# Two more weight blocks by seven products for their first K tile pair, and W1 over four PSUM banks

## The chip, the cores and the metric

The kernel runs on one core of one Trainium2 chip. The metric is the device time of one execution in microseconds, as the median over runs. One profiled execution is read beside it.

## What is computed

The reference is a decoder trunk of two layers over 256 tokens of width 2048, in float32. The first layer mixes by a gated short convolution, the second by latent attention; after each mixer and after each MLP stands a layer norm of `alpha * x + f(x)`. The change lies in the MLP alone, which both layers have:

```python
def sq_relu_mlp(x, w1, w2):
    return jnp.square(jax.nn.relu(x @ w1)) @ w2
```

x is 256 x 2048, W1 is 2048 x 8192, W2 is 8192 x 2048.

## The kernel before

**Products of float32.** TensorE multiplies a rounded format, so every operand is held as a high part (a cast on ScalarE, `split`, L122) and a low part (the rest, by a subtraction on VectorE, L123), and a product is three matmuls: high by high, high by low, low by high (`dot`, L284 to L286). In the W1 part the tokens' high and low parts stand side by side, so there a weight tile takes one matmul of 512 columns (`high`, L200) and one of 256 (`low`, L204).

**The weight stream.** All weights are a list of units in the order in which they are used (`stream`, `mlp_stream`). `take` hands out the next unit and prepares units ahead of it: a load on SP's queue (`load_raw`, L133) into one of 5 raw tiles, then the split into one of 8 pairs of high and low tiles. It looks ahead while the sizes of the units sum to at most `LOOK` = 5; a plain unit (128 x 1024) has size 1, a seven-product unit 3. A scheduler then decides the order of the instructions on each engine, each of which runs its queue in order.

**The MLP.** The 8192 hidden features are worked in 8 steps of 1024 features each (`for q in range(NQ)`): 8 chunks of W1, each 16 K tiles long (`products`), then W2 for these 8 K tiles. The sums of the W1 chunks take turns in PSUM banks 0 and 1. Each chunk is read out by `hidden`: a copy on ScalarE (L340), an add on VectorE (L341), relu and square on ScalarE (L654, L655), and for every second chunk the split of two K tiles and, in `form`, four sums of 128 x 128 blocks (L643 to L646) with their split. W2's output is two token tiles (t) by four blocks of 512 columns (n), kept in SBUF as `acc`.

**Seven products.** In the steps 1 to 6 (`FAST`) blocks 0 and 1 are computed by a scheme of Strassen's kind over 2 token tiles x 2 K tiles x 2 blocks: seven products of block sums in place of eight (`FACTORS`, `fast_products`). For each K tile pair, `prepare` forms the sums of W2's blocks on VectorE (L155, L158, L161) and splits them; such a unit has three pairs of high and low tiles and one of half the size (`t4`). `first_pair` runs the four K tile pairs into seven banks, which `keep` (L601) then adds into SBUF: three sums into `acc`, four ("1", "5", "7", "6", named `OWN`) into `sums`. After the last fast step, during step 7, `fold` (L620) adds `sums` into `acc`. Blocks 2 and 3 follow as plain products (`down`), one block after the other, four units each, evicted by `put` (L591). In the second MLP, `extra` adds the turned residual (L958) in steps 1 to 4.

So a fast step has these units in order: 16 plain units of W1, four seven-product units, eight plain units of W2.

Of the kernel before, what the change touches and what calls it, by code (L numbers as in the profile page):

```python
# [10 lines left out]
F32 = mybir.dt.float32  # L11
# [5 lines left out]
P = 128  # L17
W = 256 + 2
T = 256
# [15 lines left out]
NB = 4  # L35
BW = D // NB
FAST = range(1, NQ - 1)
FIRST = (0, 1, 2, 3, 4, 6, 8, 12, 16)
LEAD = 4
HEAD = 4  # L40
# [11 lines left out]
def trunk(ctx: ExitStack, tc: tile.TileContext, xT, vecs, lead, w_first, w_in, w_out, w_kv, w_q, w_uk, w_uv,  # L52
# [28 lines left out]
    def mlp_stream(l):  # L81
        out = []
        for q in range(NQ):
            out += halves(w1[l, q * QC:(q + 1) * QC])
            plain = halves(w2[l, q, 2:] if q in FAST else w2[l, q])
            fast = [(w2f[l, q, j, 0], w2f[l, q, j, 1]) for j in range(QC // 2)] if q in FAST else []
            at = 0 if q or q not in FAST else len(plain) // 2
            out += plain[:at] + fast + plain[at:]
        return out

    stream += mlp_stream(0) + halves(w_kv) + halves(w_q)
# [77 lines left out]

        return 1 if len(stream[i]) == 1 else 3  # L170

    def take(halves=2):

        i = state["next"]
        state["next"] += halves
        ahead = -sum(size(j) for j in range(i, i + halves))
        for j in range(i, len(stream)):
            ahead += size(j)
            if ahead > LOOK:
                break  # L180
# [92 lines left out]
    def products(n, x, turned=None, banks=(None,)):  # L273

        for i in range(n):
            w = take()
            ps = psum("ps_u", banks[i % len(banks)])
            mm_run([(w, ps)], x, 0, NC, NC, turned=None if i else turned)
            yield ps


    def dot(ps, w, x, first, last):

        nc.tensor.matmul(ps, x[0], w[0], start=first, stop=False)  # L284
        nc.tensor.matmul(ps, x[0], w[1], start=False, stop=False)  # L285
        nc.tensor.matmul(ps, x[1], w[0], start=False, stop=last)  # L286

    def held(x, t):
# [33 lines left out]
    OWN, KEPT = ("1", "5", "7", "6"), (2, 3, 4, 5, 6, 7, 0)  # L322
# [5 lines left out]
    def fast_products(ps, x, forms, j, n):  # L328

        b, = take(1)  # L330
        a = {"11": held(x[2 * j], 0), "12": held(x[2 * j + 1], 0), "22": held(x[2 * j + 1], 1)}
        for i in range(4):
            a[f"S{i + 1}"] = [forms[:, j, o, i * P:(i + 1) * P] for o in range(2)]
        for p, l, r in FACTORS:
            dot(ps[p], b[r], a[l], j == 0, j == n - 1)

    def whole(ps, out):

# [228 lines left out]
    def mlp(idx, ln, blocks, fast, begin=None, extra=None):  # L567
# [14 lines left out]
        def block(n, t):  # L582
            return acc[:, t, n * BW:(n + 1) * BW]
# [6 lines left out]
            else:  # L590
                nc.vector.tensor_tensor(block(n, t), block(n, t), ps, ALU.add)  # L591

        sums = fast.tile([P, 4, BW], F32, name=f"sums{idx}")

        def keep(p, ps):

            at = sums[:, OWN.index(p)] if p in OWN else block(*{"2": (0, 0), "3": (1, 0), "4": (0, 1)}[p])
            if q == 0 or q == FAST[0] and p in OWN:
                nc.scalar.copy(at, ps)
            else:  # L600
                nc.vector.tensor_tensor(at, at, ps, ALU.add)  # L601

        def first_pair(h, forms, banks):

            n = QC // 2
            ps = {p: psum(f"ps_f{p}", bank) for (p, _, _), bank in zip(FACTORS, banks)}
            for j in range(n):
                fast_products(ps, h, forms, j, n)
            for p in ps:
                keep(p, ps[p])  # L610

        def fold():

            s1, s5, s7, s6 = (sums[:, i] for i in range(4))
            both = acc[:, 1, :2 * BW].rearrange("p (b c) -> p b c", b=2)
            right = acc[:, :, BW:2 * BW]
            two = lambda v: v.unsqueeze(1).to_broadcast([P, 2, BW])
            for d, a, b in ((block(0, 0), block(0, 0), s1), (s6, s6, s1), (block(1, 0), block(1, 0), s6),
                            (s7, s7, s6), (both, both, two(s7)), (right, right, two(s5))):
                nc.vector.tensor_tensor(d, a, b, ALU.add)  # L620
                yield

        for q in range(NQ):
            ht = act.tile([P, QC, 2 * T], F32R, tag="c", name=f"h{idx}_{q}")
            h = [ht[:, k, :] for k in range(QC)]
            forms = None
            if q in FAST:
                forms = act.tile([P, QC // 2, 2, 4 * P], F32R, tag="a2", name=f"forms{idx}_{q}")
            pair = []

            def pair_tile(m):

                if m % 2 == 0:
                    pool = (act, "ab") if m % 4 else (fast, "fp")
                    t = pool[0].tile([P, 2 * T], F32, tag=pool[1], name="fp")
                    pair.append(t.rearrange("p (i t) -> p i t", i=2))
                return pair[-1]

            def form(j):
                (a11, a21), (a12, a22) = ((pair[j][:, i, :P], pair[j][:, i, P:]) for i in range(2))  # L640
                sf = fast.tile([P, 4, P], F32, tag="sf", name="sf")
                s1, s2, s3, s4 = (sf[:, i, :] for i in range(4))
                nc.vector.tensor_tensor(s1, a21, a22, ALU.add)  # L643
                nc.vector.tensor_tensor(s3, a21, a11, ALU.subtract)
                nc.vector.tensor_tensor(s2, s1, a11, ALU.subtract)
                nc.vector.tensor_tensor(s4, a12, s2, ALU.subtract)  # L646
                split(forms[:, j, 0, :], forms[:, j, 1, :], sf.rearrange("p i c -> p (i c)"))

            def hidden(m, ps, evac, *func):
                both = pair_tile(m) if q in FAST else None  # L650
                f = both[:, m % 2, :] if both is not None else tmp.tile([P, T], F32, tag="fh", name="fh", bufs=3)
                evac(ps, f, *func)
                if not func:
                    nc.scalar.activation(f, f, AF.Relu)  # L654
                nc.scalar.activation(f, f, AF.Square)  # L655
                if both is None:
                    put_split(h[m], f)
                elif m % 2:
                    at = ht[:, m - 1:m + 1, :]
                    split(at[:, :, :T], at[:, :, T:], both)  # L660
                    form(m // 2)

            if q == 0:
                for m in range(QC):
                    if m < GROUP:
                        if m == 0:
                            ws = ln.ws if ln.ws else group_of(GROUP)
                            if not ln.ws:
                                mm_wide(ws, ln.xd)
                            ln.finish()  # L670
                        ps = ws[m][1]
                    else:
                        ws = [(take(), psum("ps_w"))]
                        mm_wide(ws, ln.xd)
                        ps = ws[0][1]
                    hidden(m, ps, ln.weighted, AF.Relu)
                    if m > 0:
                        normal()
                if begin:
                    begin(range(1))  # L680
                acc = act.tile([P, 2, D], F32, tag="a1", name=f"acc{idx}")
            else:
                folds = fold()
                for m, ps in enumerate(products(QC, xhl, TURNED, (0, 1))):
                    hidden(m, ps, whole)
                    if q == NQ - 1:
                        next(folds, None)
                        if begin:
                            begin(range(max(2 * m, 1), 2 * m + 2))

            if q == NQ - 1:
                blocks(block, put, h)
                return
            if q == 0:
                for n in range(NB):
                    down(h, put, n)
            else:
                first_pair(h, forms, KEPT)
                for n, banks in ((2, (1, 2)), (3, (3, 4))):
                    down(h, put, n, banks)  # L700
                    if extra and n == 2 and q <= NB:
                        for t in range(2):
                            extra(block, q - 1, t, 5 + t)

    def to_wide(block, put, h):

# [409 lines left out]
```

## Time and profile before

| what | value |
|---|---|
| runs | median 2024.65 us (2024.43, 2024.65, 2025.12) |
| the profiled execution's own time | 2024.51 us |
| its span, first to last instruction | 2022.5 us |
| granted TensorE clock | 1.00 |
| HBM read | 381.78 MB |

In the rows of the profile, PE is TensorE's matmul, PEld its weight load, DVE VectorE, ACT ScalarE, SP the queue that issues the loads. A row of a group gives line, engine, operation, output<-inputs, shapes, count, busy us, mean ns of one, and the idle time just before with what ended it. A row of the timeline gives start and length in us. A row of the stretches gives its window, its length, and then for PE, PEld, DVE, ACT and POOL the busy time and the number of instructions, the clock, the DMA share and GB/s. Lines are those of the kernel before.

### The profile page before, as it was taken

The numbers are of one execution on the slowest core, as the hardware profiler recorded it, in microseconds if no ns is written. First come the engines' busy times: TensorE is split into PE (matmuls) and PEld (weight loads), VectorE is DVE, ScalarE is ACT, GpSimd is POOL, SyncE is SP. The second block draws the span as 40 slices with busy tenths as digits, with TensorE's granted clock in tenths as the row PEclk, the third lists the DMA queues.
The fourth block names the chain that finished last, engine by engine and source line by source line (L and its number), as shares of the span: only waits on it lengthen the run. The fifth ranks groups of instructions, "written<-read, shape, count | busy, mean of one in ns | idle before, by whom it ended". The sixth has DMA issues, their size and how long they took to land.

```text
span 2022.5 us, 30067 instructions
## 1 busy us (share of the span) xinstructions
PE 2015.9 (100%) x11240; PEld 1761.4 (87%) x11240; DVE 1605.8 (79%) x2472; ACT 1176.4 (58%) x1802; POOL 2.3 (0%) x21
## 2 busy tenths in 40 slices
PE   9999999999999999999999999999999999999998
PEld 8888888988888888888889998898888888888886
DVE  8667677788797987979688978776879798797966
ACT  6444445676565665656556655567656556565651
POOL 0000000000000000000000000000000000000000
PEclk9999999999999999999999999999999999999999
DMA  9666666564756647466654544656475664746663
GB/s 322 201 189 188 189 189 192 174 196 144 250 164 202 221 153 249 151 224 209 210 173 152 182 126 137 193 178 194 135 247 176 198 224 140 252 160 205 220 202 119
DMA packets 106849, 385.83 MB, mean 191 GB/s; under 512 B 11856, under 2 KB 12624, under 8 KB 106448
## 3 DMA queue, kind: packets, MB, share of 16 engines
q1 hardware_dynamic: 106560, 383.79, 59.5%
q8 instruction: 88, 1.44, 0.3%
q14 instruction: 57, 0.47, 0.1%
q10 hardware_dynamic: 144, 0.13, 0.0%
HBM read 381.78 MB, written 2.10 MB: 190 GB/s over the span
## 4 chain that ended last, share of the span: by engine, by line
PE 99%; DVE 0%; issue 0%; ACT 0%; DVEq 0%
PE ps_u L200 20%; PE ps_l L200 13%; PE ps_u L204 11%; PE ps_d L284 7%; PE ps_d L286 7%; PE ps_d L285 7%; PE ps_l L204 7%; PE ps_f L285 4%; PE ps_f L286 4%; PE ps_f L284 4%; PE ps_w L234 1%; PE ps_w L232 1%; PE ps_w L233 1%; PE ps_g L234 1%; PE ps_g L232 1%; PE ps_g L233 1%
## 5 line engine op out<-in xcount | busy, mean ns | idle before, releaser
L123 DVE TENSOR_TENSOR lo<-raw,hi 128x1024 fp32r<-128x1024 f32 x710 | 860.0, 1222 | 314.9 <-ACT hi L122 243.2
L122 ACT CAST hi<-raw 128x1024 fp32r<-128x1024 f32 x710 | 742.4, 1050 | 460.5 <-PE ps_u L200 107.9
L200 PE MATMUL ps_u<-xhl,hi 128*128 128x512 f32 x1792 | 621.0, 391 | 0.0
L204 PE MATMUL ps_u<-xhl,lo 128*128 128x256 f32 x1792 | 499.5, 280 | 0.0
L200 PEld LDWEIGHTS ps_u<-xhl,hi 128*128 128x128 f32 x1792 | 334.2, 187 | 72.4
L204 PEld LDWEIGHTS ps_u<-xhl,lo 128*128 128x128 f32 x1792 | 338.6, 189 | 1.8
L284 PE MATMUL ps_d<-hi,h 128*128 128x512 f32 x640 | 249.8, 390 | 0.0
L286 PE MATMUL ps_d<-hi,h 128*128 128x512 f32 x640 | 249.1, 389 | 0.0
L285 PE MATMUL ps_d<-lo,h 128*128 128x512 f32 x640 | 249.0, 389 | 0.0
L200 PE MATMUL ps_l<-xhl_a,hi 128*128 128x512 f32 x704 | 244.1, 393 | 0.0
L204 PE MATMUL ps_l<-xhl_a,lo 128*128 128x256 f32 x704 | 195.4, 279 | 0.0
L200 PEld LDWEIGHTS ps_l<-xhl_a,hi 128*128 128x128 f32 x704 | 132.1, 188 | 29.9
L286 PEld LDWEIGHTS ps_d<-hi,h 128*128 128x128 f32 x640 | 120.1, 188 | 25.0
L284 PEld LDWEIGHTS ps_d<-hi,h 128*128 128x128 f32 x640 | 120.1, 188 | 25.0 <-DVE fh L341 0.3
L285 PEld LDWEIGHTS ps_d<-lo,h 128*128 128x128 f32 x640 | 120.2, 188 | 24.7
L204 PEld LDWEIGHTS ps_l<-xhl_a,lo 128*128 128x128 f32 x704 | 131.9, 188 | 0.2
L654 ACT ACTIVATE fp<-fp 128x256 f32<-128x256 f32 x96 | 40.0, 416 | 73.7 <-DVE fp L341 72.9
L200 PE MATMUL ps_l<-z,hi 128*128 128x512 f32 x240 | 82.4, 391 | 0.0
L122 ACT CAST hi_t<-raw_t 128x1024 fp32r<-128x1024 f32 x48 | 50.4, 1050 | 42.2 <-DVE raw_t L155 33.4
L234 PE MATMUL ps_w<-xd,hi 128*128 128x258 f32 x256 | 72.8, 284 | 0.0
L232 PE MATMUL ps_w<-xd,hi 128*128 128x258 f32 x256 | 72.6, 284 | 0.0
L233 PE MATMUL ps_w<-xd,lo 128*128 128x258 f32 x256 | 72.4, 283 | 0.0
(261 smaller groups left out, 3132.3 us busy)
## 6 DMA issues: line engine op xcount, KB each, us to landing
raw<-in_w_dram SPq DMA_DIRECT2D x416, 512.0 KB, 4.4
raw<-in_w2f_dram SPq DMA_DIRECT2D x96, 512.0 KB, 3.6
raw<-in_w_in_dram SPq DMA_DIRECT2D x88, 512.0 KB, 4.3
raw<-in_w_out_dram SPq DMA_DIRECT2D x32, 512.0 KB, 3.7
raw<-in_w_o_dram SPq DMA_DIRECT2D x32, 512.0 KB, 4.2
raw<-in_w_kv_dram SPq DMA_DIRECT2D x10, 512.0 KB, 3.5
raw<-in_w_q_dram SPq DMA_DIRECT2D x8, 512.0 KB, 4.6
raw<-in_w_uk_dram SPq DMA_DIRECT2D x8, 512.0 KB, 4.6
```

Source lines behind the costliest of these rows:

```text
L122: nc.scalar.copy(hi, src)
L123: nc.vector.tensor_tensor(lo, src, hi.bitcast(F32), ALU.subtract)
L200: nc.tensor.matmul(ps, w[blk // 8][0][:, blk % 8, :], x, start=first, stop=False)
L204: nc.tensor.matmul(ps[:, :T], w[blk // 8][1][:, blk % 8, :], x[:, :T], start=False, stop=last)
L232: nc.tensor.matmul(ps[:, :W], hi, x[k][:, :W], start=k == 0, stop=False)
L233: nc.tensor.matmul(ps[:, :W], lo, x[k][:, :W], start=False, stop=False)
L234: nc.tensor.matmul(ps[:, :W], hi, x[k][:, W:], start=False, stop=k == NC - 1)
L284: nc.tensor.matmul(ps, x[0], w[0], start=first, stop=False)
L285: nc.tensor.matmul(ps, x[0], w[1], start=False, stop=False)
L286: nc.tensor.matmul(ps, x[1], w[0], start=False, stop=last)
L654: nc.scalar.activation(f, f, AF.Relu)
```

## The change

In the fast steps, blocks 2 and 3 take their first K tile pair by the seven products too (`MIXED = "sppp"`: s for seven, p for plain), and their other three pairs by plain products into the same sums where a sum is an output block ("2", "3", "4"; the fourth block, "22", begins with the plain pairs). W2's units of a step now come in the order: one seven-product unit of blocks 2 and 3, six plain units, four seven-product units of blocks 0 and 1. `sums` holds two sets of four. The W1 chunks take turns in four banks, and the banks of a step are handed on to the next in a rotation; the bank of the last chunk goes to "22". One middle matmul of a fast step (`EVEN`) is made in two halves of 256 columns. The plain W2 units are taken with a look-ahead of 6. `fold` has eight adds on 1024 columns in place of six. The host lays W2 out in pairs for all four blocks.

```diff
+MIXED = "sppp"
+EVEN = (QC - 1, "22")
...
-            plain = halves(w2[l, q, 2:] if q in FAST else w2[l, q])
-            fast = [(w2f[l, q, j, 0], w2f[l, q, j, 1]) for j in range(QC // 2)] if q in FAST else []
-            at = 0 if q or q not in FAST else len(plain) // 2
-            out += plain[:at] + fast + plain[at:]
+            if q not in FAST:
+                out += halves(w2[l, q])
+                continue
+            for j, kind in enumerate(MIXED):
+                out += [(w2f[l, q, 1, j, 0], w2f[l, q, 1, j, 1])] if kind == "s" else \
+                    halves(w2[l, q, 2, j]) + halves(w2[l, q, 3, j])
+            out += [(w2f[l, q, 0, j, 0], w2f[l, q, 0, j, 1]) for j in range(QC // 2)]
...
-    def take(halves=2):
+    def take(halves=2, look=LOOK):
...
-            if ahead > LOOK:
+            if ahead > look:
...
-    def dot(ps, w, x, first, last):
+    def dot(ps, w, x, first, last, two=False):
         nc.tensor.matmul(ps, x[0], w[0], start=first, stop=False)
-        nc.tensor.matmul(ps, x[0], w[1], start=False, stop=False)
+        for at in (slice(0, T), slice(T, 2 * T)) if two else (slice(None),):
+            nc.tensor.matmul(ps[:, at], x[0], w[1][:, at], start=False, stop=False)
         nc.tensor.matmul(ps, x[1], w[0], start=False, stop=last)
...
-        sums = fast.tile([P, 4, BW], F32, name=f"sums{idx}")
+        sums = fast.tile([P, 4, 2, BW], F32, name=f"sums{idx}")
-        def keep(p, ps):
+        def keep(p, g, ps):
-            at = sums[:, OWN.index(p)] if p in OWN else block(*{"2": (0, 0), "3": (1, 0), "4": (0, 1)}[p])
-            if q == 0 or q == FAST[0] and p in OWN:
+            at = sums[:, OWN.index(p), g, :] if p in OWN else \
+                block(*{"2": (2 * g, 0), "3": (2 * g + 1, 0), "4": (2 * g, 1), "22": (2 * g + 1, 1)}[p])
+            if q == FAST[0] and p in OWN:
...
-        def first_pair(h, forms, banks):
+        def down_pairs(h, forms, busy, free):
+            b2, b3, b4, b6 = free
+            b1, b5, b7, b22 = busy
+            ps = {p: psum("ps_d", bank) for p, bank in (("22", b22), ("3", b3), ("2", b2), ("4", b4))}
+            fresh = {"22", "3", "2", "4"}
+            for j, kind in enumerate(MIXED):
+                if kind == "s":
+                    first, last = j == MIXED.index("s"), j == MIXED.rindex("s")
+                    if first:
+                        ps.update({p: psum(f"ps_f{p}", bank) for p, bank in zip(OWN, (b1, b5, b7, b6))})
+                        fresh.update(OWN)
+                    fast_products(ps, h, forms, j, fresh, OWN if last else ())
+                    fresh &= {"22"}
+                    if last:
+                        for p in OWN:
+                            keep(p, 1, ps[p])
+                    continue
+                if extra and q <= NB and j == len(MIXED) - 1:
+                    for t in range(2):
+                        extra(block, q - 1, t, (b7, b6)[t])
+                for two in (((0, "2"), (1, "4")), ((1, "22"), (0, "3"))):
+                    w, = take(1, LOOK + 1)
+                    for t, p in two:
+                        for kk in range(2):
+                            k = 2 * j + kk
+                            dot(ps[p], wide_rows(w, kk), held(h[k], t), p in fresh, k == QC - 1, (k, p) == EVEN)
+                            fresh.discard(p)
+                    if j == len(MIXED) - 1:
+                        for _, p in two:
+                            keep(p, 1, ps[p])
             n = QC // 2
+            banks = b1, b5, b7, b6, b2, b4, b22
             ps = {p: psum(f"ps_f{p}", bank) for (p, _, _), bank in zip(FACTORS, banks)}
             for j in range(n):
-                fast_products(ps, h, forms, j, n)
+                fast_products(ps, h, forms, j, ps if j == 0 else (), ps if j == n - 1 else ())
             for p in ps:
-                keep(p, ps[p])
+                keep(p, 0, ps[p])
+            return (b3, b1, b5, b7), (b6, b2, b4, b22)
...
+        busy, free = (0, 1, 2, 3), (4, 5, 6, 7)
...
-                for m, ps in enumerate(products(QC, xhl, TURNED, (0, 1))):
+                for m, ps in enumerate(products(QC, xhl, TURNED, busy)):
...
-                first_pair(h, forms, KEPT)
-                for n, banks in ((2, (1, 2)), (3, (3, 4))):
-                    down(h, put, n, banks)
-                    if extra and n == 2 and q <= NB:
-                        for t in range(2):
-                            extra(block, q - 1, t, 5 + t)
+                busy, free = down_pairs(h, forms, busy, free)
```

More of the change, by code (lines that the diff above doesn't have):

```diff
@@ L320, in down_late, with fast_products @@
                 put(n, t, ps)
-    OWN, KEPT = ("1", "5", "7", "6"), (2, 3, 4, 5, 6, 7, 0)
+    OWN = ("1", "5", "7", "6")
     FACTORS = (("3", "S4", "22"), ("1", "11", "11"), ("5", "S1", "T1"), ("7", "S3", "T3"),
                ("2", "12", "21"), ("6", "S2", "T2"), ("4", "22", "T4"))
-    def fast_products(ps, x, forms, j, n):
+    def fast_products(ps, x, forms, j, fresh, ready):
         b, = take(1)
@@ L334, in fast_products @@
         for p, l, r in FACTORS:
-            dot(ps[p], b[r], a[l], j == 0, j == n - 1)
+            dot(ps[p], b[r], a[l], p in fresh, p in ready)
     def whole(ps, out):
@@ L614, in fold @@
             s1, s5, s7, s6 = (sums[:, i] for i in range(4))
[L615 to L619, printed above, removed]
+            c = acc.rearrange("p t (g b c) -> p t b g c", g=2, b=2)
@@ L620, in fold @@
+            for d, a, b in ((c[:, 0, 0], c[:, 0, 0], s1), (s6, s6, s1), (c[:, 0, 1], c[:, 0, 1], s6), (s7, s7, s6),
+                            (c[:, 1, 0], c[:, 1, 0], s7), (c[:, 1, 1], c[:, 1, 1], s7),
+                            (c[:, 0, 1], c[:, 0, 1], s5), (c[:, 1, 1], c[:, 1, 1], s5)):
                 nc.vector.tensor_tensor(d, a, b, ALU.add)
                 yield
+        busy, free = (0, 1, 2, 3), (4, 5, 6, 7)
         for q in range(NQ):
@@ L1095 @@
         "w2": np.stack([np.stack([_rows(q) for q in w.reshape(NQ, QC * P, D)]) for w in a["mlp_w2"]]),
-        "w2f": np.stack([np.stack([_pairs(q[:, :2 * BW]) for q in w.reshape(NQ, QC * P, D)]) for w in a["mlp_w2"]]),
+        "w2f": np.stack([np.stack([np.stack([_pairs(q[:, 2 * g * BW:2 * (g + 1) * BW]) for g in range(2)])
+                                   for q in w.reshape(NQ, QC * P, D)]) for w in a["mlp_w2"]]),
         "cosT": np.tile(cos, (4, 1)),
```

## The prediction

> **What bounds the kernel now.** I read the page first: its table of engines, the strip of slices and the chain that ended last.
>
> ```profile
> PE 2015.9 (100%) x11240; PEld 1761.4 (87%) x11240; DVE 1605.8 (79%) x2472; ACT 1176.4 (58%) x1802; POOL 2.3 (0%) x21
> PEclk9999999999999999999999999999999999999999
> PE 99%; DVE 0%; issue 0%; ACT 0%; DVEq 0%
> ```
>
> TensorE is never idle, at full clock, and the chain of work runs along it for 99% of the span. Busy time alone could hide waits inside pipelined matmuls, so I next read the table by stretches over one whole middle step of the first MLP (its W1 part, then its W2 part), a middle step of the second MLP, and the W1 part of the last step of the second MLP.
>
> ```profile
> 624.10:709.30 85.20, 85.20 (x437) 72.91 (x436) 71.70 (x96) 51.29 (x72) 0.00 (x0) 1.00 0.61 197
> 624.10:668.50 44.40, 44.40 (x258) 39.13 (x257) 34.58 (x52) 27.36 (x45) 0.00 (x0) 1.00 0.53 155
> 668.50:709.30 40.80, 40.80 (x182) 33.78 (x181) 37.12 (x45) 23.93 (x28) 0.00 (x0) 1.00 0.70 243
> 1580.90:1667.00 86.10, 86.10 (x446) 73.70 (x445) 72.86 (x98) 51.42 (x72) 0.00 (x0) 1.00 0.61 196
> 1923.60:1968.00 44.40, 44.40 (x258) 39.13 (x257) 26.85 (x34) 25.91 (x44) 0.00 (x0) 1.00 0.67 202
> ```
>
> The columns are TensorE, weight loads, VectorE and ScalarE. The W2 part holds 180 matmuls (182 with the two that straddle its borders) in 40.8 us: 0.227 us each. The timeline of TensorE gives the same from start to start; the 0.39 in each row is a latency that overlaps the next.
>
> ```profile
> 620.48 0.39 PE L286 MATMUL ps_d<-hi,h 128*128 128x512 f32 x1
> 620.70 0.39 PE L284 MATMUL ps_d<-hi,h 128*128 128x512 f32 x1
> 620.93 0.39 PE L285 MATMUL ps_d<-lo,h 128*128 128x512 f32 x1
> ```
>
> So the price of a matmul of 512 columns is 0.227 us (0.45 us over two starts), not 0.39, and a step is the bare sum of its matmuls. VectorE comes second: 71.70 of 85.20 us. It is the engine to watch.
>
> **What the change removes from TensorE.** Blocks 2 and 3 of a fast step took 8 K tiles x 2 blocks x 2 token tiles x 3 = 96 matmuls of 512 columns. With seven products for the first pair, that pair needs 7 x 3 = 21 in place of 24. There are 6 fast steps in each of 2 MLPs: 12 x 3 = 36 matmuls fewer, 36 x 0.227 = **8.17 us**.
>
> The Trainium skill ("TensorE: Matmul & The Clock Gate", section "Back-to-back issue gap") states a sustained 131 ns per matmul with N = 512; by that figure, as an estimate, the sum would be 4.7 us and the time 2020. The rows say 227 ns, and the measurement decides: no chance goes to it below.
>
> **What it adds there.** One middle matmul per fast step is split in two of 256 columns, so 12 instructions more. The nearest rows are runs of 258 columns, and one of 256 between two of 512:
>
> ```profile
> 361.99 0.28 PE L232 MATMUL ps_g<-xd,hi 128*128 128x258 f32 x1
> 362.11 0.28 PE L233 MATMUL ps_g<-xd,lo 128*128 128x258 f32 x1
> 362.23 0.28 PE L234 MATMUL ps_g<-xd,hi 128*128 128x258 f32 x1
> ...
> 624.33 0.28 PE L204 MATMUL ps_u<-xhl,lo 128*128 128x256 f32 x1
> 624.44 0.40 PE L200 MATMUL ps_u<-xhl,hi 128*128 128x512 f32 x1
> ```
>
> Start to start 0.12 and 0.11 us: two halves 0.24 against 0.227, so +0.01 each, 0.15 us in all with rounding up. Bounds: 0 (the halves stream the same columns) to a whole further slot, 12 x 0.227 = 2.7 us. I take 0.15, which the rows give nearly directly. The trace has no odd run of matmuls to tell what the split is for. The order of the rest (mixed pair, six plain units, four seven-product units) moves no matmul between stages: each step still changes from W1 to W2 work once and back once.
>
> The sum on TensorE: -8.17 + 0.15 = **-8.0 us**, if it stays fed.
>
> **What feeds it: VectorE.** Its queue is in order; each weight tile is cast high on ScalarE, then subtracted on VectorE. The rows of one seven-product unit in the step above (its first tile was subtracted before them):
>
> ```profile
> 676.22 1.22 DVE L155 TENSOR_TENSOR raw_t<-raw,raw 128x1024 f32<-128x1024 f32 x1
> 677.35 0.29 DVE L646 TENSOR_TENSOR sf<-fp,sf 128x128 f32<-128x128 f32 x1
> 677.55 0.69 DVE L158 TENSOR_TENSOR raw<-raw,raw_t 128x512 f32<-128x512 f32 x1
> 678.28 0.69 DVE L161 TENSOR_TENSOR raw<-raw 128x512 f32<-128x512 f32 x1
> 678.88 1.22 DVE L123 TENSOR_TENSOR lo_t<-raw_t,hi_t 128x1024 fp32r<-128x1024 f32 x1
> 680.02 0.69 DVE L123 TENSOR_TENSOR forms<-sf,forms 128x512 fp32r<-128x512 f32 x1
> 680.62 1.22 DVE L123 TENSOR_TENSOR lo<-raw,hi 128x1024 fp32r<-128x1024 f32 x1
> 681.76 0.68 DVE L123 TENSOR_TENSOR t<-raw,t 128x512 fp32r<-128x512 f32 x1
> 682.36 3.68 DVE L123 TENSOR_TENSOR lo<-raw,hi 128x1024 fp32r<-128x1024 f32 x3
> ...
> 690.79 1.28 DVE L601 TENSOR_TENSOR sums<-sums,ps_f 128x512 f32<-128x512 f32 x2
> ```
>
> Start to start, 1024 columns take 1.14, 512 take 0.60, 128 take 0.20 us (an eviction of 512 too: two of 0.68 in 1.28). A unit of seven products has four of 1024 (its third high-low tile among them) and three of 512: 4 x 1.14 + 3 x 0.60 = 6.36 us. It stands for two plain units of 1.14, so +4.1. The evictions rise from 11 to 15 a step: +2.4. Together +6.5 us: 71.7 becomes 78.2 of 84.5 us, 93%. That is still below TensorE, so VectorE takes no more than its idle 13.5 us; what counts is the place. ScalarE gains one cast of 1024 (1.05 us below) and one of 512, under 2 us on 51.3: covered by some 30 us of idle time. Loads stay 32 a step and only change their order in SP's queue; the look-ahead of 6 moves plain units earlier in the queues and adds nothing.
>
> ```profile
> L122 ACT CAST hi<-raw 128x1024 fp32r<-128x1024 f32 x32 | 33.5, 1050 | 20.9 <-DMA raw<-in_w_dram 9.1 <-PE ps_u L200 6.9 <-PE ps_d L286 3.0
> L341 DVE TENSOR_TENSOR fp<-ps_u,t 128x256 f32<-128x256 f32 x8 | 3.3, 418 | 0.0
> ```
>
> The place is the W2 part. Let 0 be the start of the mixed unit. TensorE takes 21 x 0.227 = 4.8 us for it and 12 x 0.227 = 2.7 for each plain unit; the four last units begin at 21.1, 25.9, 30.6 and 35.4, and all ends at 40.2. VectorE, in the order in which the changed kernel has its queue: the add of the last W1 chunk at about 2.8 (at 0 its last tile's buffer comes free, then one cast on ScalarE and one on VectorE of 1.1 to 1.2 each, then the add of 0.42), and behind it four new evictions, whose sums end at 1.4, 2.0, 2.7 and 4.1: done at 5.6. These waits hold up nothing that is due: the six plain units are cast by then but one. Then one plain cast, the last forms and hidden tile (1.4), four units less one subtraction made earlier (24.3) and four evictions (2.4): 5.6 + 29.2 = about 35. The last unit's subtracted tile is ready at about 33.7 and first read at 35.4 + 6 x 0.227 = 36.8: **3.1 us of room**, the tightest place. Its last tile, ready at 35, is read at 39.5. The next step's first W1 tiles follow at 37 (read at 40.2).
>
> The buffers allow it. With eight high-low tiles, the third of the last four units writes its last tile at about 28 and needs the first unit read (25.9); the fourth at about 34, after the second is read (30.6). With five raw tiles, a unit's loads start when the unit two before it is cast, 6 us ahead:
>
> ```profile
> raw<-in_w_dram SPq DMA_DIRECT2D x416, 512.0 KB, 4.4
> raw<-in_w2f_dram SPq DMA_DIRECT2D x96, 512.0 KB, 3.6
> ```
>
> 3.6 to 4.4 us to land lie beside those 6. The banks: W1 with four banks instead of two leaves a chunk 4 x 5.5 us until its bank returns; the last chunk's bank is wanted by the sum that begins at 7.5 and is read out by about 3. I cost both at nothing; without that cover the late add (2.8) would fall on TensorE, at most 12 x 2.8 us.
>
> The last step folds eight times 1.14 instead of 4 x 0.60 + 2 x 1.14: +4.4 us on 26.85 of 44.40, one fold a chunk: hidden. The second MLP's transposes (86.1 against 85.2) only move ahead of the last two plain units, with their two reads of 0.6 on VectorE: the room shrinks to about 2.6 us there.
>
> So the profiled execution, 2024.51 us around a span of 2022.5, becomes 2016.5; the median of the runs stands 0.14 above it: **2016.6 us**.
>
> **Rivals.** *Handovers make VectorE late (slower).* Where VectorE waits for ScalarE's cast, the trace shows:
>
> ```profile
> 700.14 1.22 DVE L123 TENSOR_TENSOR lo<-raw,hi 128x1024 fp32r<-128x1024 f32 x1 [0.60 <-ACT hi L122]
> ...
> 705.50 1.23 DVE L123 TENSOR_TENSOR lo<-raw,hi 128x1024 fp32r<-128x1024 f32 x1 [0.24 <-ACT hi L122]
> ```
>
> Four units have four handovers each, 14 up to the tightest place. At 0.30 each they cost 4.2, which is 1.1 us over the room: 12 x 1.1 - 8.0 = +5.2, 2029.9 us; at 0.60, 5.3 over, 2080. It decides from (3.1 + 0.67) / 14 = 0.27 us. For it: VectorE at 93%, and evictions that wait for sums now stand amid its casts. Against: in the unit quoted above the gaps are 0.13 and 0, about 0.05 a handover, 0.7 in 14, since other work fills them; and in the rows quoted the wait was for loads or for buffers still being read, which is VectorE being ahead. The Trainium skill ("TensorE: Matmul & The Clock Gate", section "Architectural detail: the array is 16× 32×32, not 1× 128×128") calls VectorE's and ScalarE's queues strict FIFO; the order of the rows agrees, and this is why a late eviction would delay casts.
>
> *Edges.* The split costs its upper bound, 2.7 us, or small waits where units change: -5.4, 2019.2 us. For it: nothing in the trace has this split. Against: the 0.12 rows.
>
> *It all comes back (no change).* VectorE's room is used up to just 0.67 us of stall a step: 2024.6. This needs the handover case to stop near its point of decision.
>
> **How the numbers follow.** Forecast (2015.7 to 2018): 0.75. Edges (2018 to 2021.5): 0.08. No change: 0.05. Handovers: 0.12, above 2028.7 in all of it. The range 2015.7 to 2021.5 holds the first two, 0.83; its lower end is no price for the split and 0.7 us of spread. A measurement tells about 0.2% (4 us) from no change, so faster means under 2020.6: 0.75 and most of the edges, 0.81; slower 0.12; same 0.07.
>
> **What would show it.** Right: 11216 matmuls instead of 11240 (48 fewer of 512 columns, 24 more of 256), a W2 part of 40.2 us with 178 matmuls, W1 parts of 44.4, VectorE at about 78 a step, no idle time ahead of weight loads in W2. Wrong: a W2 part over 40.8 us; weight loads of the last seven-product units released by VectorE; casts idle behind evictions. What would make it wrong is a wait in VectorE's queue that the row of before has no counterpart for, above all the new evictions between casts.

## The result, and the profile after

The changed kernel takes **2018.34 us** in the median of 8 runs (2017.18 to 2019.81) beside 2024.67 us for the kernel before in the same measurement (8 runs, 2024.43 to 2025.12): a ratio of 0.9969, with a 95% interval of 0.9959 to 0.998. Forecast were 2016.6 us, and 2015.7 to 2021.5 as the range. So it is faster by 6.3 us where 8.0 were expected, and the runs differ by 2.6 us where those of before differ by 0.7.

In the profile after, lines have moved: the matmuls of W2 (`dot`) are L289, L291 and L292, the split's casts L127 and L128, the three block sums of a seven-product unit L160, L163 and L166, the add of a W1 chunk L347, the evictions (`keep`) L608. From the page, the engines, the clock, the chain and the loads of the seven-product units:

```profile
PE 2008.4 (100%) x11216; PEld 1755.4 (87%) x11216; DVE 1687.5 (84%) x2576; ACT 1194.4 (59%) x1834; POOL 2.3 (0%) x21
PEclk9999999999999999999999999999999999999999
PE 98%; DVE 1%; DMA 0%; issue 0%; ACT 0%; DVEq 0%
raw<-in_w2f_dram SPq DMA_DIRECT2D x120, 512.0 KB, 4.2
```

11216 matmuls are the number forecast. The chain is no longer TensorE alone: VectorE and, new in the list, DMA are in it. The table by stretches shows three parts of the first MLP in a row (the W2 part of its fifth fast step, the next W1 part, the next W2 part; columns as in the prediction):

```profile
836.60:876.80 40.20, 40.20 (x181) 33.24 (x180) 37.77 (x48) 20.27 (x27) 0.00 (x0) 1.00 0.42 132
876.80:921.20 44.40, 44.40 (x258) 39.13 (x257) 39.80 (x56) 31.86 (x47) 0.00 (x0) 1.00 0.76 257
921.20:962.30 41.10, 40.57 (x179) 33.06 (x179) 38.52 (x50) 20.65 (x27) 0.00 (x0) 1.00 0.40 131
```

The first W2 part is what the prediction wanted: 40.20 us, TensorE never idle. VectorE has 77.6 us in the 84.6 of a step, 92%. The third is longer and has idle time on TensorE. It is the only W2 part of this execution that loses more than 0.1 us, and this execution is the fastest of the 8 runs.

The sum of the profiled execution comes out of the W2 parts, from the first matmul of each to the first of the next W1 part: 40.84 us before and 40.20 after in eight fast steps, 41.73 to 41.77 before and 41.10 after in the four with the turned residual. 8 x 0.64 + 4 x 0.65 = 7.7 us gained; 1.0 lost in the disturbed part; 0.4 more gained outside the W2 parts of the fast steps: 7.1, which is the difference of the spans (2022.5 and 2015.4).

Where that part lost its time stands in its waits, in TensorE's row and in VectorE's timeline:

```profile
DVE raw_t L160 <- DMA raw<-in_w2f_dram: 2.4, 1, 2.4
PEld ps_f L289 <- issue: 0.9, 1, 0.9
PE ps_f L289 <- DVE acc L608: 0.5, 1, 0.5
PEld ps_f L291 <- DVE lo_t L128: 0.3, 1, 0.3
```

```profile
946.16 0.39 PE L292 MATMUL ps_f<-hi,forms 128*128 128x512 f32 x1
947.08 0.47 PE L289 MATMUL ps_f<-t,h 128*128 128x512 f32 x1 [0.53 <-DVE acc L608]
```

```profile
921.55 1.22 DVE L128 TENSOR_TENSOR lo<-raw,hi 128x1024 fp32r<-128x1024 f32 x1
922.69 0.28 DVE L682 TENSOR_TENSOR sf<-fp 128x128 f32<-128x128 f32 x1
925.38 1.23 DVE L160 TENSOR_TENSOR raw_t<-raw,raw 128x1024 f32<-128x1024 f32 x1 [2.41 <-DMA raw<-in_w2f_dram]
926.52 1.22 DVE L128 TENSOR_TENSOR lo<-raw,hi 128x1024 fp32r<-128x1024 f32 x1
927.66 0.42 DVE L347 TENSOR_TENSOR fp<-ps_u,t 128x256 f32<-128x256 f32 x1
927.99 1.87 DVE L608 TENSOR_TENSOR sums<-sums,ps_f 128x512 f32<-128x512 f32 x3
929.82 0.29 DVE L681 TENSOR_TENSOR sf<-fp 128x128 f32<-128x128 f32 x1
930.03 0.68 DVE L608 TENSOR_TENSOR sums<-sums,ps_f 128x512 f32<-128x512 f32 x1
...
957.77 1.22 DVE L128 TENSOR_TENSOR lo_t<-raw_t,hi_t 128x1024 fp32r<-128x1024 f32 x1
```

Read it from the top, with 921.15 as time 0. At 1.8 VectorE comes to the first subtraction (L160) of the first of the four last units and waits until 4.2 for the second of that unit's two loads. Everything behind it in the queue waits too, though it could run: a plain weight's low part, the add of the last W1 chunk (at 6.5, where I had put 2.8) and the four evictions (done at 9.6, not 5.6). The delay runs through the queue. At 25.9 TensorE stands 0.7 us before a product whose bank an eviction frees too late; the last unit's subtracted tile, forecast at 33.7, is ready at 37.8.

Why the load is late shows in the chain of that window:

```profile
919.48 1.23 DVE lo L128
920.71 0.02 issue
920.73 4.53 DMA raw<-in_w2f_dram
925.26 0.03 issue
```

The load needs a raw tile. It gets the one that this subtraction of a plain weight has just read (done at 920.71), and lands 4.53 us later.

The group of this subtraction says how much of this there is in the whole execution. Before, it is L155; after, L160:

```profile
L155 DVE TENSOR_TENSOR raw_t<-raw,raw 128x1024 f32<-128x1024 f32 x48 | 58.5, 1220 | 5.4 <-DMA raw<-in_w2f_dram 5.2
L160 DVE TENSOR_TENSOR raw_t<-raw,raw 128x1024 f32<-128x1024 f32 x60 | 73.3, 1221 | 27.6 <-DMA raw<-in_w2f_dram 27.4
```

**The theory**: this wait at the head of VectorE's in-order queue is what separates 2018.3 from the forecast. In the six fast steps of the first MLP L160 starts 1.2, 2.4, 3.0, 3.3, 3.2 and 4.2 us after the mixed unit, and only the last of these steps loses more than 0.1 us: up to about 3.3 the room pays. **The rivals**: VectorE is simply too full, at 92%, wherever the subtraction stands; or the new order, the split or the banks cost something by themselves.

### The profile page after: what moved, and what is told of

It reads as the page before. It is cut to its first block, busy times and chain, and to the rows that moved or that the text cites. A ratio compares the mean times of both kernels' runs of the same rounds, so it can differ in the third digit from the quotient of the medians.

```text
span 2015.4 us, 30041 instructions
## 1 busy us (share of the span) xinstructions
PE 2008.4 (100%) x11216; PEld 1755.4 (87%) x11216; DVE 1687.5 (84%) x2576; ACT 1194.4 (59%) x1834; POOL 2.3 (0%) x21
## 4 chain that ended last, share of the span: by engine, by line
PE 98%; DVE 1%; DMA 0%; issue 0%; ACT 0%; DVEq 0%
PE ps_u L205 20%; PE ps_l L205 13%; PE ps_u L209 11%; PE ps_l L209 7%; PE ps_d L292 6%; PE ps_d L291 6%; PE ps_d L289 6%; PE ps_f L291 4%; PE ps_f L289 4%; PE ps_f L292 4%; PE ps_w L239 2%; PE ps_w L237 2%; PE ps_w L238 2%; PE ps_g L237 1%; PE ps_g L239 1%; PE ps_g L238 1%
## 5 line engine op out<-in xcount | busy, mean ns | idle before, releaser
L128 DVE TENSOR_TENSOR lo<-raw,hi 128x1024 fp32r<-128x1024 f32 x710 | 861.3, 1220 | 199.6 <-ACT hi L127 128.8
L127 ACT CAST hi<-raw 128x1024 fp32r<-128x1024 f32 x710 | 740.5, 1050 | 379.0 <-PE ps_l L205 97.8
L289 PE MATMUL ps_d<-hi,h 128*128 128x512 f32 x556 | 217.2, 391 | 0.0
L292 PE MATMUL ps_d<-hi,h 128*128 128x512 f32 x556 | 216.6, 390 | 0.0
L291 PE MATMUL ps_d<-lo,h 128*128 128x512 f32 (+1 forms) x568 | 216.4, 385 | 0.0
L291 PEld LDWEIGHTS ps_d<-lo,h 128*128 128x128 f32 x568 | 106.7, 188 | 22.0
L292 PEld LDWEIGHTS ps_d<-hi,h 128*128 128x128 f32 x556 | 104.4, 188 | 21.4
L289 PEld LDWEIGHTS ps_d<-hi,h 128*128 128x128 f32 x556 | 104.4, 188 | 21.0
L127 ACT CAST hi_t<-raw_t 128x1024 fp32r<-128x1024 f32 x60 | 62.9, 1048 | 85.5 <-DVE raw_t L160 78.9
L160 DVE TENSOR_TENSOR raw_t<-raw,raw 128x1024 f32<-128x1024 f32 x60 | 73.3, 1221 | 27.6 <-DMA raw<-in_w2f_dram 27.4
L128 DVE TENSOR_TENSOR lo_t<-raw_t,hi_t 128x1024 fp32r<-128x1024 f32 x60 | 73.1, 1218 | 0.0
L239 PE MATMUL ps_w<-xd,hi 128*128 128x258 f32 x256 | 72.8, 284 | 0.0
```

What stands on the lines that cost most here:

```text
L127: nc.scalar.copy(hi, src)
L128: nc.vector.tensor_tensor(lo, src, hi.bitcast(F32), ALU.subtract)
L160: nc.vector.tensor_tensor(t.rearrange(two, a=2), b12.unsqueeze(1).to_broadcast([P, 2, BW]), r1.rearrange(two, a=2), ALU.subtract)
L239: nc.tensor.matmul(ps[:, :W], hi, x[k][:, W:], start=False, stop=k == NC - 1)
L291: nc.tensor.matmul(ps[:, at], x[0], w[1][:, at], start=False, stop=False)
```

## The experiments

Each ratio is to the kernel before, with its 95% interval; no kernel leaves work out. The kernel before, measured again beside each, has medians of 2024.64 to 2024.86 us, so medians are also compared with one another.

### The changed kernel again

> The changed kernel once more, for a second profile and more times. Theory (late loads): in each fast step VectorE stands about 2.3 us at the head of its queue, waiting for the second load of the first of the four last units, because five raw tiles let that load start too late; this uses up the room in the W2 part, and how much TensorE then stalls (0 to 2.5 us in all) depends on the latency of a few loads in that run. Expected: median 2018.3, runs spread over about 2.5 us as before, the wait of 2.2 to 2.5 us in nearly all 12 steps, and stalls of TensorE in other steps than the sixth of the first MLP. Rival (fixed price): the missing time is a cost of the split or of edges, the same in each run; then the same stalls stand at the same places.

2018.91 us (10 runs, 2017.03 to 2023.76), 0.9974 (0.9965 to 0.9983). The profiled execution is the slowest, 2023.76. Its page has this chain, and its third W2 part these stretch and waits:

```profile
PE 73%; DVE 16%; DMA 6%; issue 3%; ACT 2%; SPq 0%; DVEq 0%; ACTq 0%
```

```profile
668.30:710.20 41.90, 40.96 (x180) 33.08 (x179) 39.55 (x51) 21.65 (x29) 0.00 (x0) 1.00 0.43 135
```

```profile
DVE raw_t L160 <- DMA raw<-in_w2f_dram: 2.2, 1, 2.2
PEld ps_f L289 <- issue: 1.3, 1, 1.3
PE ps_f L289 <- DVE acc L608: 0.9, 1, 0.9
PEld ps_d L289 <- DVE fp L347: 0.4, 1, 0.4
```

Now seven fast steps are disturbed, the one of before (by 0.2 us) and six others. In the seven, L160 starts 3.5 to 5.1 us after the mixed unit; in the five undisturbed ones, 1.2 to 2.2. Where it is latest (4.9 here, 5.1 in the second MLP) the late add holds up the sum "22" as well (the last row): the cover under which I had priced the banks at nothing is gone. So the loss is no fixed price of the new work: in the W2 parts of these two profiles the same program loses 1.0 us or 7.2, and it loses where L160 starts late. Two things were expected otherwise: the waits of L160 at this place are 1.3 to 3.2 us and not 2.2 to 2.5 in nearly all steps, and the runs spread over 6.7 us and not 2.5.

### Without the split matmul

> Without the split of one middle matmul into halves (177 matmuls in a W2 part in place of 178). By the 0.12 and 0.11 us rows of before the split costs 0.01 us each: 0.1 us less in all, 2018.2, W2 parts of 40.18. If the split is there to keep the number of matmuls even and that matters, W1 parts that follow get longer than 44.39 us, and the kernel is slower by the sum of it.

```diff
-EVEN = (QC - 1, "22")
+EVEN = None
```

2017.70 us (6 runs, 2015.93 to 2019.15), 0.9967 (0.9955 to 0.9979). The W2 part has 177 matmuls and takes 40.16 us where it had 178 and 40.20; the W1 parts stay at 44.39. So the split costs 0.04 us a step, 0.5 in all (0.15 forecast), and an odd number of matmuls harms nothing here. The spread stays at 3 us: it isn't the split that makes the runs differ.

### The order and the banks alone

> The new order of units, the bank rotation with four banks for W1 and the look-ahead, but no mixed unit and no split: all four K tile pairs of blocks 2 and 3 plain, so 180 matmuls in a W2 part and 11 evictions as before the change. If order and banks by themselves cost and bring nothing: 2024.6 us, W2 parts of 40.84, VectorE at about 72 us of 85.2 a step, a spread under 1 us. If the order itself makes VectorE late, stalls of TensorE and a spread of 2 us as in the changed kernel.

```diff
-MIXED = "sppp"
-EVEN = (QC - 1, "22")
+MIXED = "pppp"
+EVEN = None
```

(with `fold` over blocks 0 and 1 alone). 2030.12 us (8 runs, 2028.65 to 2031.39), 1.0026 (1.0016 to 1.0036): slower than before by 5.3 us. Now "22" begins in the second plain unit, 2.7 us after the first, in the bank of the last W1 chunk, and TensorE waits there for the late add (`PE ps_d L289 <- DVE fp L347`): each W2 part is 0.1 to 0.8 us longer than before. I had priced this part of the change at nothing. Whether the order itself or the queue is to blame is asked again below.

### The last chunk's bank to a sum that begins at once

> The bank of the last W1 chunk goes to sum 1, which begins 0.7 us after the mixed unit, and the first of the four W1 banks to the sum that begins last. Late loads: the add that reads out the last chunk ends 6 us after the mixed unit begins, since it stands in VectorE's queue behind the subtraction that waits for its load; TensorE waits for it 5 to 6 us in each of 12 steps: 2080 to 2090 us. As predicted blind (the add at 2.8 us): 2 to 2.5 us a step, 2043 to 2048.

```diff
-            b1, b5, b7, b22 = busy
+            b22, b5, b7, b1 = busy
```

2030.98 us (5 runs, 2030.21 to 2031.43), 1.0031 (1.0019 to 1.0043), 12.6 above the change. TensorE stands 0.3 to 1.1 us in every step but one at product "1" of the mixed unit, until the add of the last chunk is done, and 3.2 us in that one. Both expectations were too high. They took product "1" to be due 0.7 us after the start of the unit; in the run the scheduler has put it behind other products, where it is due at 3.0. And VectorE is less late than the first of them assumed: L160 has the same place in its queue, waits 0.8 to 1.6 us for its load (2.1 in the one step), and the add is done at 3.3 to 4.1 (6.2 in that step). So giving the last chunk's bank to "22" is worth 12.6 us with the rest in place.

### W1 over two banks

> W1's chunks alternate between the third and fourth of the four banks alone (the rest of the rotation as changed). The first chunk of the next step then goes to a bank whose last eviction ends 3.3 us after it should begin (in the profile after, the second eviction of the last units ends at 880.1, W1 begins at 876.8): 2 to 3.3 us of stall at each of 12 borders, some of it given back because VectorE catches up meanwhile: 2040 to 2056 us. If four banks are no help: 2018.3.

```diff
-                for m, ps in enumerate(products(QC, xhl, TURNED, busy)):
+                for m, ps in enumerate(products(QC, xhl, TURNED, busy[2:])):
```

2041.02 us (4 runs, 2038.27 to 2043.0), 1.0079 (1.0066 to 1.0093). At 11 of the 12 borders to the next W1 part TensorE waits 0.4 to 2.7 us for an eviction of the last units:

```profile
626.85 0.39 PE L292 MATMUL ps_f<-t,h 128*128 128x512 f32 x1
628.41 0.47 PE L205 MATMUL ps_u<-xhl,hi 128*128 128x512 f32 x1 [1.17 <-DVE sums L608]
```

Four banks are worth 22.7 us: they let the next W1 part begin in banks that were read out long before. The waits at the borders are about 15 of the 23.5 us between the two profiled spans; the rest lies in W1 parts of up to 46.8 us instead of 44.39, and only a part of that is explained (last section).

### Two mixed units

> Two of the four K tile pairs of blocks 2 and 3 by seven products: 36 matmuls fewer again (-7.7 us at 0.214 net as measured), VectorE +4.1 us a step to about 82.3 of 83.1. By the rates alone 2010.6. If VectorE's lateness is carried from step to step, it becomes the bound: 1 to 4 us of stall a step, 2022 to 2055 us.

```diff
-MIXED = "sppp"
+MIXED = "sspp"
```

2023.92 us (10 runs, 2020.55 to 2028.36), 0.9996 (0.9987 to 1.0005). An undisturbed W2 part is 39.52 us (40.42 with the turned residual), as three matmuls fewer give, but only the first of each MLP is undisturbed; others take up to 44.2, with TensorE waiting 1.3 us at a time for `lo_t`, the last unit's subtracted tile. VectorE has 81.6 us of work in one such step (623.2 to 710.4), which without stalls would take 83.9. So one unit further than the change goes, TensorE is no longer fed. That VectorE's work alone does this isn't shown: L160 waits for its load here too, up to 3.3 us, and no run has two mixed units with the subtraction behind the add.

### The subtraction on GpSimd

> The first subtraction of each seven-product unit (1024 columns, five a step) is made on GpSimd in place of VectorE: VectorE falls from 78 to 72.5 us a step with the same loads, tiles and order of units. If VectorE at 93% is what cannot make up lateness: TensorE unstalled, 2016.6 to 2016.9, spread under 1 us. If late loads alone do it: still 2018.3 with stalls, since the instruction that needs the subtraction's result still stands in the same place. A danger: GpSimd may take several us for it, more than the 1.14 of VectorE, and slow VectorE meanwhile.

```diff
-        nc.vector.tensor_tensor(t.rearrange(two, a=2), ...
+        nc.gpsimd.tensor_tensor(t.rearrange(two, a=2), ...
```

2120.05 us (5 runs, 2117.49 to 2125.45), 1.048 (1.0466 to 1.0494). The group of L160, now on GpSimd:

```profile
L160 POOL TENSOR_TENSOR raw_t<-raw,raw 128x1024 f32<-128x1024 f32 x60 | 176.6, 2943 | 1545.6 <-DMA raw<-in_w2f_dram 684.0 <-DVE fp L347 429.1 <-issue 223.3
```

2.94 us instead of 1.22, and it is in the middle of each unit: the other two sums and three casts wait for it. VectorE's queue is freed of the wait, but each unit becomes late. The test says nothing for or against the theory.

### Six raw tiles

> Six raw tiles in place of five; to make room, the tile of half size (t4) of a seven-product unit has one buffer in place of two. Late loads: the wait ahead of the first subtraction falls from 2.3 us to under 0.5, TensorE no longer stalls in the W2 parts (40.2 us each), 2016.8 to 2017.2 us, and the spread of the runs falls to under 0.8 us. Rival (VectorE's sheer work at 93% makes it late): still 2018.3 with the same spread. Rival (fixed price): no change. A danger: the single t4 buffer makes VectorE wait for the last product of the unit before, which would show as waits of the t4 cast for TensorE.

```diff
-RAW, WA = 5, 8
+RAW, WA = 6, 8
...
-        f = state["fast"].tile([P, 2, BW], F32R, tag="t4", name=f"t4_{i}", bufs=2)
+        f = state["fast"].tile([P, 2, BW], F32R, tag="t4", name=f"t4_{i}", bufs=1)
```

The sixth raw tile takes the room of the second `t4`. 2019.33 us (8 runs, 2018.69 to 2021.2), 0.9975 (0.9965 to 0.9985): no gain. But its profile (the 2018.69 run) has L160 at 2.0 to 1.2 us *before* the mixed unit, and ten of twelve W2 parts undisturbed at 40.20 and 41.10. What it loses lies in the first fast step of each MLP, and the larger of these two has the same form on another engine:

```profile
535.99 1.05 ACT L127 CAST hi<-raw 128x1024 fp32r<-128x1024 f32 x1 [1.16 <-DMA raw<-in_w_dram]
536.95 0.61 ACT L127 CAST t<-raw 128x512 fp32r<-128x512 f32 x1
```

```profile
538.95 0.50 PE L291 MATMUL ps_f<-t,h 128*128 128x512 f32 x1 [0.84 <-DVE t L128]
```

ScalarE waits for the load of a W1 tile that is due later, with the `t` that TensorE wants next behind it in its queue. The danger named beforehand shows as well: the casts into `t4` wait 5.5 us in all for TensorE's reads, where the changed kernel has no such wait. So this run supports the cause by its stretches but doesn't prove it by the time: neither the median nor the spread (2.5 us) came out as the theory forecast.

### Seven raw tiles and seven pairs

> Seven raw tiles and seven pairs of high and low tiles instead of five and eight; all else as in the changed kernel. Theory (the wait at the head of VectorE's queue comes from the raw tile that is free too late): the first subtraction starts at 0 or before, without a wait for its load, and stalls of that kind are gone; 2016.2 to 2017.5. Rival (seven pairs are too few for four seven-product units in a row): ScalarE's casts wait for TensorE's reads in the W2 part, stalls of 0.3 to 1 us a step in the last units, 2020 to 2030.

```diff
-RAW, WA = 5, 8
+RAW, WA = 7, 7
```

2020.47 us (10 runs, 2018.98 to 2021.02), 0.9978 (0.9969 to 0.9987), in neither theory's way. In its profile L160 stands 1.2 to 2.1 us ahead of the mixed unit, its waits fall from 27.6 to 6.9 us in all, and all twelve W2 parts are undisturbed:

```profile
L160 DVE TENSOR_TENSOR raw_t<-raw,raw 128x1024 f32<-128x1024 f32 x60 | 73.2, 1220 | 6.9 <-DMA raw<-in_w2f_dram 6.7
```

The last W2 part begins at 1960.43, 0.45 before that of the change's profile, but the end comes 57.8 us later instead of 54.5: 3.3 us are lost there. In the last layer norm the scheduler has another order on VectorE, and TensorE's last six products (`offset`) wait 3.0 us for it instead of 1.2; then they take 4.2 us instead of 2.8, at a granted clock of 0.67 instead of 1.00; the other 0.2 us are in the W2 part. The median says "no gain", the stretches say that the cause is gone and something else was spoilt.

### The subtraction behind the add

> The changed kernel with one order set by hand: the first subtraction (L160) of the first of the four last units is issued behind the add of the last W1 chunk (L347) on VectorE; the scheduler then puts it behind the four evictions too, in all steps but the first of each MLP. Work, tiles and loads are the same. Theory (the subtraction waits for its load at the head of VectorE's queue and holds up the add and the evictions): the add at about 3, the evictions done at about 6, the subtraction waits less than 0.4 us for its load, no stall in the 12 W2 parts, each 40.20 (41.10 with the turned residual): median 2016.2 to 2017.0, runs within 1.5 us of each other. Rival one (VectorE at 93% is simply too full, wherever the subtraction stands): stalls and spread as in the changed kernel, 2018 to 2019. Rival two (the later subtraction makes its own unit late): stalls where the first of the four last units begins, above 2020.

```diff
-        two = "p (a c) -> p a c"
-        nc.vector.tensor_tensor(t.rearrange(two, a=2), b12.unsqueeze(1).to_broadcast([P, 2, BW]),
-                                r1.rearrange(two, a=2), ALU.subtract)
+        with tc.issue_after(state.pop("mark")) if "mark" in state else nullcontext():
+            nc.vector.tensor_tensor(t.rearrange("p (a c) -> p a c", a=2), b12.unsqueeze(1).to_broadcast([P, 2, BW]),
+                                    r1.rearrange("p (a c) -> p a c", a=2), ALU.subtract)
...
-        nc.vector.tensor_tensor(out, ps[:, :T], t, ALU.add)
+        state["add"] = nc.vector.tensor_tensor(out, ps[:, :T], t, ALU.add).ins
...
-            b1, b5, b7, b22 = busy
+            (b1, b5, b7, b22), state["mark"] = busy, state["add"]
```

`issue_after` sets an order on one engine's queue and adds no wait. Work, tiles and loads are those of the change.

**2016.19 us** (5 runs, 2016.04 to 2016.34), 0.9959 (0.9945 to 0.9972). All five lie below the lowest of the change's 18 runs (2017.03), and the spread is 0.3 us. The chain, and VectorE in the step that was disturbed in the change (time 0 is 921.20):

```profile
PE 100%; DVE 0%; issue 0%; DVEq 0%
```

```profile
923.51 0.42 DVE L347 TENSOR_TENSOR fp<-ps_u,t 128x256 f32<-128x256 f32 x1
923.85 1.87 DVE L608 TENSOR_TENSOR sums<-sums,ps_f 128x512 f32<-128x512 f32 x3
925.67 0.29 DVE L681 TENSOR_TENSOR sf<-fp 128x128 f32<-128x128 f32 x1
925.88 0.68 DVE L608 TENSOR_TENSOR sums<-sums,ps_f 128x512 f32<-128x512 f32 x1
...
930.36 1.22 DVE L160 TENSOR_TENSOR raw_t<-raw,raw 128x1024 f32<-128x1024 f32 x1
...
955.01 1.22 DVE L128 TENSOR_TENSOR lo_t<-raw_t,hi_t 128x1024 fp32r<-128x1024 f32 x1
```

The add is at 2.3, the evictions are done at 5.4 (forecast: 2.8 and 5.6), L160 finds its tile loaded, and the last unit's subtracted tile is ready at 35.0, 1.8 us before its read at 36.8. All twelve W2 parts take 40.20 or 41.10. VectorE has as much work as in the change (1685.8 and 1687.5 us of busy time), so the rival "too full" falls: the wait at the head of the queue costs 2018.34 - 2016.19 = 2.15 us in the median.

### The same without the split

> The same without the matmul that is made in two halves. Theory: W2 parts of 40.16 with 177 matmuls and no stalls, so 0.04 x 12 = 0.5 us below the run with the split, 2015.7 to 2016.5. Rival (the even number of matmuls matters for what follows): W1 parts longer than 44.39, and not below the run with the split.

2016.0 us (5 runs, 2015.34 to 2016.13), 0.9957 (0.9945 to 0.997). All W2 parts are 40.16 or 41.06, undisturbed. In time it can't be told from the run with the split. These two are the best versions here.

### The order alone, the subtraction behind the add

> The order and the four banks alone (no seven-product unit in blocks 2 and 3, no matmul in two halves), with the first subtraction of the four last units issued behind the add of the last W1 chunk. Here the sum on the last chunk's bank begins with the second plain unit, at 2.7, and the add was done at 2.3 to 2.7 in the run with the seven-product unit and the subtraction behind it. Theory (the order and the banks cost nothing of their own; what the order alone cost, 5.3 us, is the same wait at the head of VectorE's queue): stalls at 3 of at most 0.3 us a step, 2024.3 to 2027. Rival (the order costs by itself, through casts or loads): stalls of 0.3 to 0.7 us a step as without the edit, 2029 to 2031.

2026.29 us (10 runs, 2025.86 to 2026.5), 1.0007 (0.9998 to 1.0017). Of the 5.3 us that the order cost above, the queue's wait was about three quarters: the W2 parts, 40.99 to 42.57 us there, come down to an even 40.99, or 41.90 with the turned residual. What is left, 0.15 us a step over before, is one short wait at 3.1, where "22" begins in the second unit, just before the add is done:

```profile
PEld ps_d L289 <- DVE fp L347: 0.3, 1, 0.3
```

The mixed unit removes this too, since "22" then begins at 7.5. The run before this one differs by the mixed unit (with its sums in `fold`) alone, and is 10.3 us faster: 8.2 by the matmuls and 12 x 0.15 = 1.8 by this wait make 10.0 of it.

## Why the prediction was right, and where it wasn't

The sign, the range and the mechanism of the gain held; that TensorE stays fed did not, so the size was 1.7 us too good, and the likeliest case's own range (2015.7 to 2018) was missed by 0.3. The median falls into the bracket called "edges", by small waits and not by the split. That it stayed in the range is partly luck: the sum had no term for the wait, which costs 1.0 us in one profile and 7.2 in the other, and one of the 18 runs (2023.76) lies above the range.

- **36 matmuls fewer, 8.17 us, and the split, 0.15.** Right: 11216 matmuls, W2 parts shorter by 0.64 and 0.65 where the sum gave 0.67. The split was 0.5 us, not 0.15. Without stalls the kernel takes 2016.19, 0.4 from the forecast.
- **VectorE 71.7 to 78.2 us a step.** Right: 77.6.
- **"The add of the last W1 chunk at about 2.8" and "3.1 us of room".** This is the step that failed. The arithmetic is right for the queue that I drew (2.3 and 5.4 measured with the subtraction behind the add), but in the changed kernel that subtraction stands *ahead* of the add. I counted its 1.14 us as "made earlier" and gave it no wait. It waits 1.4 to 2.4 us for its load (up to 3.2 in the slowest profile), with the add and the evictions behind it. The room was about 0: in an undisturbed step (836.57) the tile read at 36.8 was ready at 36.8.
- **"A unit's loads start when the unit two before it is cast, 6 us ahead."** It holds for the three later units, which find their tiles loaded in every fast step but the first. For the first of the four, the tile that its second load needs is freed by a plain weight just before: at 920.71, for a subtraction that VectorE reaches at 923.0, and the load takes 4.5 us. So the lead was 2.3 us and not 6.
- **"I cost both [banks] at nothing."** Right only under its cover, as the text said: with a late add the sum "22" waits (0.2 and 0.4 us in two steps of the slowest profile), and with the last chunk's bank given to product "1" 12.6 us are lost.
- **Rivals.** Handovers: wrong place. In the run with the subtraction behind the add the stretch from the end of the evictions to the last subtracted tile takes 29.7 us; the sum was 28.1, and 1.14 of the difference is the subtraction that moved in. So the handovers cost at most 0.5 us. "A wait in VectorE's queue that the row of before has no counterpart for" was named as what would make the forecast wrong, though the evictions were suspected and a load was the cause.

What stays open: why the lateness builds up from step to step in the first MLP (1.2 to 4.2 us in the first profile) and mostly not in the second (1.2 to 1.5), and so why runs of one program differ by several us.

## What to carry to other kernels

When a step's room is summed up, walk the in-order queue entry by entry and ask of each when its *last* input lands; an instruction that is early in the queue and late in its data costs everything behind it, while its own unit isn't even due. A busy share of 92% was affordable as soon as the idle 8% stood nowhere in front of due work: one changed order gave in the median what two more raw tiles gave in the stretches alone. When an experiment removes a cause and the median doesn't move, compare stretch by stretch before the theory is dropped.

## What the runs showed of the hardware

TensorE's granted clock fell after idle times of a few us. With the subtraction on GpSimd, two waits of 2.2 and 2.3 us with three matmuls between them were followed by matmuls at twice their price. Stretches just before and after (the column after GpSimd's is the granted clock), and TensorE's rows:

```profile
700.00:708.00 8.00, 6.24 (x29) 4.86 (x27) 4.60 (x7) 2.64 (x4) 4.93 (x2) 1.00 0.45 131
713.00:718.00 5.00, 5.00 (x15) 3.95 (x15) 3.95 (x5) 1.66 (x2) 0.05 (x1) 0.59 0.48 178
```

```profile
713.09 0.63 PE L289 MATMUL ps_f<-t,h 128*128 128x512 f32 x1
713.52 0.63 PE L291 MATMUL ps_f<-t,h 128*128 128x512 f32 x1
```

0.43 us from start to start instead of 0.227, at a granted clock of 0.59. In other runs one wait was enough: 3.1 us at 590.26 in the run with the last chunk's bank given to product "1", 2.6 us at 541.02 with W1 over two banks. In that same run a wait of 2.2 us at 716.27 left the clock at 1.00:

```profile
590.00:594.00 4.00, 3.74 (x10) 3.02 (x11) 3.59 (x8) 2.88 (x5) 0.00 (x0) 0.60 0.43 131
541.00:545.00 4.00, 3.98 (x15) 3.48 (x16) 3.81 (x5) 4.00 (x6) 0.00 (x0) 0.62 0.98 397
716.20:720.00 3.80, 3.73 (x21) 3.30 (x22) 3.21 (x4) 3.04 (x4) 0.00 (x0) 1.00 1.02 415
```

Stalls of 0.3 to 1.1 us, as in the change, left the clock at 1.00 too. The Trainium skill ("TensorE: Matmul & The Clock Gate", section "Wait — 56ns, not 53.3ns?") gives 426.7 ns for 512 columns on a cold array, and the rows agree.

The same float32 subtraction of 128 x 1024 took 2.94 us on GpSimd and 1.22 on VectorE, 2.4 times as long. The Trainium skill ("GPSIMD Engine Reference", section "3.1 Elementwise — side-by-side cycle accounting") has a ratio of 1.96 for an add of 2048 columns; this operation of 1024 columns did worse, and no run here shows why.
